# A second, transposed copy of the memory in a one-core encoder layer: its row factors spread by two matmuls with ones instead of sixteen transposes of its rows

## Chip, cores and metric

The kernel runs on one core of one Trainium2 chip. The metric is device time in microseconds (us) of one launch; less is better. Before the change three runs gave 854.33 to 855.25 us, median 854.94 us.

## What is computed

One layer of a bidirectional encoder trunk on 512 tokens of width 1024: token mixing (an attention group beside an HGRN2 group with gated scans), cross-attention into 256 memory tokens, a gated MLP with a convolution. Every sub-layer has an RMSNorm ahead and behind. Cut to the part that the change touches:

```
def rmsnorm(x, g):
    y = x * rsqrt(mean(x * x, axis=-1) + EPS)
    return y * g
...
m = rmsnorm(mem, mem_norm_g[l])                    # mem: 256 x 1024
x = x + rmsnorm(memory_cross_attention(h, m, w_xq[l], w_xkv[l], w_xo[l]), post_x_g[l])
...
kv = (m @ wkv)                                     # keys and values of the cross-attention
```

The whole program is one `layer` function in float32; products are kept at nearly float32 accuracy by splitting each operand into a rounded high part and a low part.

## The kernel before

**Products.** A projection multiplies activations by weight units of 128x1024. Every operand is held as a pair of fp32r tiles, high and low, made by `split` (lines 102 to 104): a copy on ACT (line 103) and a subtraction on DVE or POOL (line 104). `mm3` (lines 145 to 148) issues the three products high-high, high-low and low-high, so the lines 146, 147 and 148 of PE are the projections of the whole kernel. `issue` (line 115) loads a weight unit over SP and splits it, three units ahead of its use.

**Order.** The kernel is recorded in program order and a scheduler places the instructions on each engine by priorities and by its own idea of durations; every engine then runs its list strictly in order. `weave` (line 57) decides the recording order by shares: in the mixing stage (line 630) it interleaves `mix_projections` (line 607) with `cores` (line 618), the HGRN2 cores of heads 0 to 2. PE has the projections to do while a core's chain on DVE goes on.

**A core** (`hgrn_core`, line 439) begins with a sum of two key tiles on DVE (line 449) and four float32 matmuls on it (line 452). Then come levels m = 1, 2, 4, ... 64: ACT copies the keys (line 459), PE makes four float32 matmuls (line 462), DVE scales keys and queries in place (line 488, twice), multiplies decay factors (line 493) and merges the result under a mask (line 494). A level's matmuls need the DVE scalings of the level before and the ACT copy behind them. Its products go to the two PSUM banks of tag "c"; its copies use a ring of four tiles of tag "th" (`TMP_BUFS`, line 40).

**The memory.** `mem_norm` (line 592), called first in `mix_projections`, loads the gain row, spread over 128 partitions, and the two 128x1024 blocks of rows. `row_rstd` (line 197) squares and sums a block on ACT (line 199), POOL makes the reciprocal root (lines 164, 165), and `scale_rows` (line 180) multiplies rows by factor and gain on DVE in two halves (line 181, four instructions in all). `mem_turn` (line 602), called after the projections of head 2, transposes the 16 blocks of 128x128 on PE (`turn_in`, line 184; matmuls against the identity, line 190) in four groups of four, each into a PSUM bank of tag "b", and splits each bank into the pair `kv["m"]`, which the key and value projections of the cross-attention read much later. Right after it `mix_projections` goes on with the attention's keys and values (`put_kv`, line 555: rotary tables at lines 529 and 531, `vv` splits, `norm_rope`).

Of the kernel before, what the change touches and what calls it, by code (L numbers as in the profile page):

```python
# [9 lines left out]
F32 = mybir.dt.float32  # L10
F32R = mybir.dt.float32r
BF16 = mybir.dt.bfloat16
U8 = mybir.dt.uint8
ACT = mybir.ActivationFunctionType
ALU = mybir.AluOpType
# [3 lines left out]
P = 128  # L19
D = 1024  # L20
T = 512
NB = T // P
KC = D // P
M = 256
MB = M // P
# [48 lines left out]
def layer(tc, io, out):  # L74
    nc = tc.nc
    ctx = ExitStack()
    pool = lambda name, **k: ctx.enter_context(tc.tile_pool(name=name, **k))
    const = pool("const", bufs=1)
# [8 lines left out]
    def small():  # L87
        return sm.tile([P, 16], F32, name="small", tag="small")

    def bank(tag):  # L90
        return ps.tile([P, 512], F32, name="ps_" + tag, tag=tag)

    def big(shape, dt=F32):
        return b8.tile(shape, dt, name="big", tag="big")

    def tmp2(shape=(P, 512), dt=F32, tag="ta"):
        return t2.tile(list(shape), dt, name="tmp2", tag=tag, bufs=TMP_BUFS[tag])

    def tmp4(shape, dt=F32):
        return t4.tile(shape, dt, name="tmp4", tag="tmp4")  # L100

    def split(hi, lo, src, eng=None):
        nc.scalar.copy(hi, src)  # L103
        (eng or nc.vector).tensor_sub(lo, src, hi.bitcast(F32))  # L104
# [45 lines left out]
    def blk(b):  # L150
        return slice(b * P, (b + 1) * P)

    def rows_bc(src, n):
        return src[None, :].to_broadcast([P, n])

    def gains(*names, eng=None):
        g = big([P, 2, D])
        for i, name in enumerate(names):
            (eng or nc.gpsimd).dma_start(g[:, i, :], rows_bc(io[name], D))
        return [g[:, i, :] for i in range(len(names))]  # L160

    def rstd_of(ss, n, width):
        r = small()
        nc.gpsimd.tensor_scalar(r[:, :n], ss, 1.0 / width, EPS, op0=ALU.mult, op1=ALU.add)
        last_pow[0] = nc.gpsimd.tensor_tensor(out=r[:, :n], in0=r[:, :n], in1=nhalf[:, :n], op=ALU.pow).ins
        return r

    def half(c):
        return slice(c * 512, c * 512 + 512)
# [10 lines left out]
    def scale_rows(xb, r, g, h, c):  # L180
        nc.vector.scalar_tensor_tensor(out=h[:, half(c)], in0=xb[:, half(c)], scalar=r, in1=g[:, half(c)],
                                       op0=ALU.mult, op1=ALU.mult)

    def turn_in(h, act, b, tags, before=None):
        for c in range(2):
            if before:
                before(c)
            o = bank(tags[c]).rearrange("p (k n) -> p k n", k=4)
            for k in range(4):
                nc.tensor.transpose(o[:, k, :], h[:, blk(c * 4 + k)], ident)  # L190
            hi, lo = act.hi, act.lo
            if len(hi) == 2:
                split(hi[c][:, :, blk(b)], lo[c][:, :, blk(b)], o)
            else:
                split(hi[0][:, c * 4:c * 4 + 4, blk(b)], lo[0][:, c * 4:c * 4 + 4, blk(b)], o)

    def row_rstd(xb, h):
        ss = small()
        nc.scalar.activation(h, xb, ACT.Square, accum_out=ss[:, 0:1])
        return rstd_of(ss[:, 0:1], 1, D)[:, 0:1]  # L200
# [111 lines left out]
    ident = const.tile([P, P], F32, name="ident")  # L312
    g_row = tmp4([P, D])
    ones = const.tile([P, P], F32, name="ones")
# [28 lines left out]
    for b in range(NB):  # L343
        h = tmp4([P, D])
        if b == 0:
            ss = small()
# [3 lines left out]
            r = ss[:, R:R + 1]  # L350
        else:
            with tc.issue_after(last_pow[0]):
                r = row_rstd(x[b], h)
        for c in range(2):
            nc.vector.scalar_tensor_tensor(out=h[:, half(c)], in0=x[b][:, half(c)], scalar=r, in1=g_pre[c],
                                           op0=ALU.mult, op1=ALU.mult)
# [233 lines left out]
    kv = {}  # L590

    def mem_norm():
        g_mem, = gains("mem_norm_g")
        kv["rows"] = big([P, MB, D])
        for b in range(MB):
            m = kv["rows"][:, b, :]
            nc.gpsimd.dma_start(m, io["mem"][blk(b), :])
            r = row_rstd(m, tmp4([P, D]))
            for c in range(2):
                scale_rows(m, r, g_mem, m, c)  # L600

    def mem_turn():
        kv["m"] = Act([big([P, 8, M], F32R)], [big([P, 8, M], F32R)])
        for b in range(MB):
            turn_in(kv["rows"][:, b, :], kv["m"], b, "bb")

    def mix_projections():
        mem_norm()
        yield from proj_tm(hT, tm_tags, put_sg)
        yield from hgrn_in(1)  # L610
        yield from hgrn_in(2)
        mem_turn()
        yield from proj_tm(hT, tm_tags, put_kv, 256)
        late = []
        yield from proj_tm(hT, tm_tags, lambda b, z: late.append(lambda: put_qn(b, z)))
        yield from hgrn_in(3, late)
# [252 lines left out]
    for b in range(NB):  # L869
        ss, done = small(), []  # L870
# [99 lines left out]
```

## Time and profile before

| what | value |
|---|---|
| three runs, median (lowest to highest) | 854.94 us (854.33 to 855.25) |
| span of the profiled execution, first to last instruction | 852.5 us |
| median of the runs less that span | 2.4 us |
| PE busy | 832.2 us, 98% of the span |
| DVE busy | 516.3 us, 61% |
| ACT busy | 395.4 us, 46% |
| POOL busy | 104.8 us, 12% |
| DMA moved | 81.43 MB, mean 96 GB/s |

The page gives the profiled execution's span; of what lies around it the page has no figure of that execution alone, so sums are made against the span of 852.5 us, and the 2.4 us by which the median of the runs stands above it are added at the end. Times in rows count from the start of the span. In a row of a timeline the first number is the start, the second the time covered, then engine, line, operation, output<-input, shapes and count; brackets give the idle time ahead of it and what ended it. Matmuls are pipelined, so the distance of two starts, and not the printed duration, is what one of them costs PE.

### The profile page before, as it was taken

What the parts mean: (1) busy time and instruction counts of PE and PEld (TensorE: products, weight loads), DVE (VectorE), ACT (ScalarE), POOL (GpSimd) and SP (SyncE); (2) the same over time, 40 slices, a digit from 0 to 9 for tenths busy, and PEclk for the clock granted to TensorE, in tenths of its full rate; (3) what the DMA queues carried; (4) which work ended last, traced back from release to release, by engine and by line L of the source; (5) the groups of instructions that cost most, each with busy time, mean ns of one, the idle gap of its engine ahead of it and who ended that gap; (6) DMA issues with size and microseconds to landing.
All of it is one profiled execution on the core that took longest, in us unless ns stands there. A gap on an engine that the chain in (4) does not pass through costs nothing.

```text
span 852.5 us, 11064 instructions
## 1 busy us (share of the span) xinstructions
PE 832.2 (98%) x4324; PEld 703.2 (82%) x4324; DVE 516.3 (61%) x780; ACT 395.4 (46%) x701; POOL 104.8 (12%) x138
## 2 busy tenths in 40 slices
PE   6999999999999999999999999999999999999996
PEld 4878889887898888888888898888888888888885
DVE  4449487969997784864453765555555556822224
ACT  6353444444888874645543643333333335511121
POOL 5210300113334401300000400000000000000001
PEclk9999999999999999999999999999999999999999
DMA  6621212122222225152212142332322222322312
GB/s 210 220 100 50 75 49 88 50 75 75 67 82 75 75 73 200 58 190 75 83 47 93 54 145 100 99 99 99 100 99 99 99 93 81 101 97 99 99 49 100
DMA packets 23894, 81.43 MB, mean 96 GB/s; under 512 B 3041, under 2 KB 3681, under 8 KB 23842
## 3 DMA queue, kind: packets, MB, share of 16 engines
q1 hardware_dynamic: 22034, 75.35, 26.0%
q0 software_dynamic: 1232, 4.46, 1.6%
q10 hardware_dynamic: 576, 0.92, 0.3%
q8 instruction: 34, 0.56, 0.3%
q14 instruction: 18, 0.15, 0.1%
HBM read 78.61 MB, written 2.10 MB: 95 GB/s over the span
## 4 chain that ended last, share of the span: by engine, by line
PE 90%; DVE 6%; ACT 2%; issue 1%; POOL 1%; DMA 0%; POOLq 0%; DVEq 0%; SPq 0%; ACTq 0%
PE ps_b L146 9%; PE ps_b L147 9%; PE ps_b L148 9%; PE ps_s L148 6%; PE ps_s L146 6%; PE ps_s L147 6%; PE ps_o L146 6%; PE ps_o L148 6%; PE ps_o L147 6%; PE ps_c L146 4%; PE ps_c L148 4%; PE ps_c L147 4%; PE ps_c L462 3%; PE ps_o L683 2%; DVE big L488 1%; PE ps_o L671 1%
## 5 line engine op out<-in xcount | busy, mean ns | idle before, releaser
L104 DVE TENSOR_TENSOR wl<-raw,wh 128x1024 fp32r<-128x1024 f32 x114 | 139.5, 1223 | 230.7 <-ACT wh L103 230.5
L103 ACT CAST wh<-raw 128x1024 fp32r<-128x1024 f32 x130 | 136.8, 1052 | 252.5 <-PE ps_o L148 85.4
L146 PE MATMUL ps_b<-big,wh 128*128 128x512 f32 (+1 forms) x320 | 117.9, 368 | 0.0
L147 PE MATMUL ps_b<-big,wh 128*128 128x512 f32 (+1 forms) x320 | 116.6, 364 | 0.0
L148 PE MATMUL ps_b<-big,wl 128*128 128x512 f32 (+1 forms) x320 | 116.5, 364 | 0.0
L174 POOL TENSOR_SCALAR small<-small 128x1 f32<-128x1 f32 x42 | 14.4, 343 | 444.9 <-ACT tmp L205 421.7
L148 PEld LDWEIGHTS ps_b<-big,wl 128*128 128x128 f32 x320 | 60.3, 189 | 9.3
L147 PEld LDWEIGHTS ps_b<-big,wh 128*128 128x128 f32 x320 | 60.4, 189 | 9.0
L146 PEld LDWEIGHTS ps_b<-big,wh 128*128 128x128 f32 x320 | 60.3, 189 | 9.0
L146 PE MATMUL ps_s<-wh,big 128*128 128x512 f32 (+1 forms) x156 | 60.8, 390 | 1.7 <-ACT big L103 1.7
L148 PE MATMUL ps_s<-wh,big 128*128 128x512 f32 (+1 forms) x156 | 60.2, 386 | 0.0
L147 PE MATMUL ps_s<-wl,big 128*128 128x512 f32 (+1 forms) x156 | 60.0, 384 | 0.0
L146 PE MATMUL ps_o<-wh,big 128*128 128x512 f32 (+1 forms) x140 | 53.9, 385 | 0.0
L148 PE MATMUL ps_o<-wh,big 128*128 128x512 f32 (+1 forms) x140 | 53.4, 382 | 0.0
L147 PE MATMUL ps_o<-wl,big 128*128 128x512 f32 (+1 forms) x140 | 53.2, 380 | 0.0
L488 DVE TENSOR_TENSOR big<-big 128x512 f32<-128x512 f32 x64 | 49.8, 786 | 3.1 <-PE ps_c L462 1.2
L104 POOL TENSOR_TENSOR wl<-raw,wh 128x1024 fp32r<-128x1024 f32 x16 | 38.7, 2423 | 58.0 <-ACT wh L103 52.7
L104 DVE TENSOR_TENSOR big<-ps_o,big 128x512 fp32r<-128x512 f32 x52 | 35.7, 688 | 15.9 <-ACT big L103 15.6
L103 ACT CAST big<-ps_o 128x512 fp32r<-128x512 f32 x52 | 30.4, 585 | 19.8 <-PE ps_o L780 7.5
L146 PE MATMUL ps_b<-wh,big 128*128 128x512 f32 x92 | 36.7, 399 | 0.0
L147 PE MATMUL ps_b<-wl,big 128*128 128x512 f32 x92 | 36.1, 393 | 0.0
L148 PE MATMUL ps_b<-wh,big 128*128 128x512 f32 x92 | 35.9, 390 | 0.0
(227 smaller groups left out, 1840.6 us busy)
## 6 DMA issues: line engine op xcount, KB each, us to landing
raw<-in_w_dram SPq DMA_DIRECT2D x132, 512.0 KB, 3.2
big<-in_x_dram SPq DMA_DIRECT2D x7, 512.0 KB, 8.8
big<-in_mem_dram POOLq DMA_DIRECT2D x2, 512.0 KB, 7.0
out_dram<-big SPq DMA_DIRECT2D x4, 256.0 KB, 2.0
out_dram<-big ACTq DMA_DIRECT2D x3, 256.0 KB, 2.0
big<-in_x_dram SPq DMA_DIRECT2D x2, 256.0 KB, 2.9
big<-in_mem_norm_g_dram POOLq DMA_DIRECT2D x1, 512.0 KB, 6.2
big<-in_post_mix_g_dram POOLq DMA_DIRECT2D x1, 512.0 KB, 6.0
```

The lines of the kernel that those rows point to most:

```text
L103: nc.scalar.copy(hi, src)
L104: (eng or nc.vector).tensor_sub(lo, src, hi.bitcast(F32))
L146: nc.tensor.matmul(o, a[0], b[0], start=start, stop=False)
L147: nc.tensor.matmul(o, a[0], b[1], start=False, stop=False)
L148: nc.tensor.matmul(o, a[1], b[0], start=False, stop=stop)
L174: nc.gpsimd.tensor_scalar(ss[:, i + 4:i + 5], ss[:, i:i + 1], 1.0 / D, ss[:, i + 3:i + 4] if i else EPS, op0=ALU.mult, op1=ALU.add)
L462: nc.tensor.matmul(o[:, b, :], kc[:, blk(b)], pat(qk, b * P, [[2 * m, P // (2 * m)], [T + m, 2], [1, m]]), start=True, stop=True)
L488: nc.vector.tensor_tensor(out=c, in0=c, in1=pat(tt, toff + off, [[2, npair], [gap, 2], [0, m]]), op=ALU.mult)
L671: nc.tensor.transpose(o[:, c, :], e[:, 0, blk(c)], ident)
L683: nc.tensor.matmul(o, vv[:, c, h // 4].rearrange("p a d -> p (a d)"), pt[:, j, c, :], start=c + j == 0, stop=c == 3 and j == 1)
```

## The change

`mem_norm` now loads the memory twice, as rows and in transposed layout (`mt`, prepared on the host as 128 x 8 x 256), and the gain as a 128x8 column tile `gm` in place of the spread row. The sums of squares of both blocks go into one small tile and one pair of POOL instructions makes both factors. No row is scaled. `mem_turn` lets POOL write two diagonal matrices of the factors (`diag`, from the "th" ring), PE multiplies ones with them (two float32 matmuls, which leave the 256 factors on every partition), ACT copies the result to `wide` (also "th"), DVE multiplies each of the eight 128x256 pieces of `mt` by its gain column and `wide` in place, and two splits of 128x1024 make the pair.

```
     def mem_norm():
-        g_mem, = gains("mem_norm_g")
-        kv["rows"] = big([P, MB, D])
+        gm = const.tile([P, KC], F32, name="gm")
+        mt, rows = big([P, KC, M]), big([P, MB, D])
+        nc.gpsimd.dma_start(gm, io["gm"])
+        nc.gpsimd.dma_start(rows, io["mem"].rearrange("(b p) d -> p b d", p=P))
+        nc.gpsimd.dma_start(mt, io["mt"])
+        ss = small()
         for b in range(MB):
-            m = kv["rows"][:, b, :]
-            nc.gpsimd.dma_start(m, io["mem"][blk(b), :])
-            r = row_rstd(m, tmp4([P, D]))
-            for c in range(2):
-                scale_rows(m, r, g_mem, m, c)
+            nc.scalar.activation(tmp4([P, D]), rows[:, b, :], ACT.Square, accum_out=ss[:, b:b + 1])
+        r = rstd_of(ss[:, :MB], MB, D)
+        kv["rows"] = mt, gm, r
 
     def mem_turn():
-        kv["m"] = Act([big([P, 8, M], F32R)], [big([P, 8, M], F32R)])
+        mt, gm, r = kv["rows"]
+        m = big([P, 8, M], F32R), big([P, 8, M], F32R)
+        kv["m"] = Act([m[0]], [m[1]])
+        diag = tmp2((P, MB, P), tag="th")
         for b in range(MB):
-            turn_in(kv["rows"][:, b, :], kv["m"], b, "bb")
+            nc.gpsimd.tensor_scalar(diag[:, b, :], ident, r[:, b:b + 1], None, op0=ALU.mult)
+        o = bank("b")[:, :M]
+        for b in range(MB):
+            nc.tensor.matmul(o[:, blk(b)], ones, diag[:, b, :], start=True, stop=True)
+        wide = tmp2((P, M), tag="th")
+        nc.scalar.copy(wide, o)
+        for kc in range(KC):
+            nc.vector.scalar_tensor_tensor(out=mt[:, kc, :], in0=mt[:, kc, :], scalar=gm[:, kc:kc + 1], in1=wide,
+                                           op0=ALU.mult, op1=ALU.mult)
+        for c in range(2):
+            k = slice(4 * c, 4 * c + 4)
+            split(m[0][:, k, :], m[1][:, k, :], mt[:, k, :])
```

On the host `arrays["mt"]` and `arrays["gm"]` are added and `mem_norm_g` is dropped. In the changed file the lines behind the edit stand 16 lower.

The scheduler places other instructions differently too. Three places follow.

**DVE where the core of head 0 begins** (line 449 is its first step, line 181 scales the memory's rows), as a piece of the difference:

```order
-L181 SCALAR_TENSOR_TENSOR big<-big,small 128x512 x4
-L449 TENSOR_TENSOR tmp_515<-big 128x512
+L449 TENSOR_TENSOR tmp_508<-big 128x512
 L493 TENSOR_TENSOR big<-big 128x512
 L488 TENSOR_TENSOR big<-big 128x256x2
 L493 TENSOR_TENSOR big<-big 128x256
-L104 TENSOR_TENSOR wl<-raw,wh 128x1024
+L493 TENSOR_TENSOR big<-big 128x128
+L493 TENSOR_TENSOR big<-big 128x64
 L488 TENSOR_TENSOR big<-big 128x256x2
```

The four row scalings ahead of the core are gone, and a weight split (line 104) that stood inside its first level now stands two levels later. On PE the core's first matmuls (line 452) have moved up accordingly: they stood behind the 7th product of `put_sg`'s second weight unit, and now stand behind the 19th of the 24 products of its first.

**DVE where the core of head 2 begins**, `mem_turn`'s work just ahead of it. Before:

```order
L429 TENSOR_TENSOR big<-tmp_889,big 128x512
L104 TENSOR_TENSOR big<-ps_b,big 128x4x128 x2
L104 TENSOR_TENSOR big<-ps_c,big 128x512
L104 TENSOR_TENSOR big<-ps_b,big 128x4x128
L449 TENSOR_TENSOR tmp_1187<-big 128x512
L104 TENSOR_TENSOR big<-ps_b,big 128x4x128
L488 TENSOR_TENSOR big<-big 128x256x2
L493 TENSOR_TENSOR big<-big 128x512
L493 TENSOR_TENSOR big<-big 128x256
L488 TENSOR_TENSOR big<-big 128x256x2
```

And now (line 617 scales `mt`, the line 104 on 128x1024 with output `big` splits it, the line 104 on `ps_c` is an output of head 1's core):

```order
L429 TENSOR_TENSOR big<-tmp_882,big 128x512
L617 SCALAR_TENSOR_TENSOR big<-big,gm,tmp_1124 128x256 x8
L104 TENSOR_TENSOR big<-big 128x1024
L104 TENSOR_TENSOR big<-ps_c,big 128x512
L104 TENSOR_TENSOR big<-big 128x1024
L449 TENSOR_TENSOR tmp_1172<-big 128x512
L493 TENSOR_TENSOR big<-big 128x512
L488 TENSOR_TENSOR big<-big 128x256x2
L493 TENSOR_TENSOR big<-big 128x256
L104 TENSOR_TENSOR wl<-raw,wh 128x1024
L488 TENSOR_TENSOR big<-big 128x256x2
```

Ten instructions on the memory now stand ahead of the core's first step where three stood (a fourth stood behind it), and a weight split has come into its first level.

**PE in the core of head 2** (line 462 are the four matmuls of a level; the lines 146 to 148 on 128x256 are the products of `put_kv`'s projection). Before, the fourth level's neighbourhood:

```order
L146 MATMUL ps_o<-wh,big 128x256
L147 MATMUL ps_o<-wl,big 128x256
L462 MATMUL ps_c<-big,tmp_1386 128x128 x4
L148 MATMUL ps_o<-wh,big 128x256
L146 MATMUL ps_s<-wh,big 128x512
```

And now:

```order
L146 MATMUL ps_o<-wh,big 128x256
L147 MATMUL ps_o<-wl,big 128x256
L148 MATMUL ps_o<-wh,big 128x256
L462 MATMUL ps_c<-big,tmp_1227 128x128 x4
L462 MATMUL ps_c<-big,tmp_1325 128x128 x4
L462 MATMUL ps_c<-big,tmp_1371 128x128 x4
L146 MATMUL ps_s<-wh,big 128x512
```

Before, the 52 products of 128x256 that follow the core's line 452 were spread between its levels: 9 ahead of the second level, 19 ahead of the third, 23 ahead of the fourth, one behind. Now 40 of them stand ahead of line 452, 12 between the first and the second level, and none between the second, the third and the fourth.

## Rows read from the trace of the kernel before

**Rows 1.** The page, part 1: busy time of PE and DVE, share, count.
```profile
PE 832.2 (98%) x4324; PEld 703.2 (82%) x4324; DVE 516.3 (61%) x780; ACT 395.4 (46%) x701; POOL 104.8 (12%) x138
```
**Rows 2.** What PE waited for: us in total, times, longest.
```profile
PE ps_c L452 <- DVE tmp L449: 2.4, 2, 1.3
```
**Rows 3.** Windows: length, then busy (count) of PE, PEld, DVE, ACT, POOL, PEclk, DMA, GB/s.
```profile
60.00:80.00 20.00, 18.50 (x105) 15.24 (x105) 19.00 (x32) 7.06 (x10) 1.86 (x3) 1.00 0.15 50
...
140.00:160.00 20.00, 19.66 (x155) 18.67 (x154) 18.39 (x37) 9.92 (x18) 2.89 (x5) 1.00 0.20 67
```
**Rows 4.** Timeline of DVE where head 0's core begins.
```profile
58.80 0.69 DVE L429 TENSOR_TENSOR big<-tmp,big 128x512 f32<-128x512 f32 x1
60.21 1.41 DVE L181 SCALAR_TENSOR_TENSOR big<-big,small 128x512 f32<-128x512 f32 x2 [0.73 <-POOL small L165]
...
63.39 0.69 DVE L449 TENSOR_TENSOR tmp<-big 128x512 f32<-128x512 f32 x1
```
**Rows 5.** Timeline of PE in the same stretch.
```profile
59.82 0.39 PE L146 MATMUL ps_o<-wh,big 128*128 128x512 f32 x1
...
64.23 1.13 PE L452 MATMUL ps_c<-tmp,tmp 128*128 128x128 f32 x8 [1.30 <-DVE tmp L449]
...
66.38 0.53 PE L147 MATMUL ps_s<-wl,big 128*128 128x512 f32 x1
...
68.28 1.20 PE L462 MATMUL ps_c<-big,tmp 128*128 128x128 f32 x8 [0.21 <-DVE big L488]
```
**Rows 6.** Timeline of PE from the first memory transposes to the fourth level of head 2.
```profile
140.87 0.60 PE L190 MATMUL ps_b<-ident,big 128*128 128x128 f32 x4
...
148.19 1.16 PE L452 MATMUL ps_c<-tmp,tmp 128*128 128x128 f32 x8
149.19 1.49 PE L462 MATMUL ps_c<-big,tmp 128*128 128x128 f32 x8
150.38 0.42 PE L148 MATMUL ps_o<-wh,big 128*128 128x256 f32 x1
...
152.03 1.20 PE L462 MATMUL ps_c<-big,tmp 128*128 128x128 f32 x8 [0.28 <-DVE big L488]
...
156.15 0.36 PE L146 MATMUL ps_o<-wh,big 128*128 128x256 f32 x1
...
158.99 1.13 PE L462 MATMUL ps_c<-big,tmp 128*128 128x128 f32 x8
...
160.08 0.40 PE L146 MATMUL ps_s<-wh,big 128*128 128x512 f32 x1
```
**Rows 7.** Timeline of DVE from the first memory split to the rotary tables.
```profile
144.79 1.28 DVE L104 TENSOR_TENSOR big<-ps_b,big 128x512 fp32r<-128x512 f32 x2
...
147.46 0.68 DVE L449 TENSOR_TENSOR tmp<-big 128x512 f32<-128x512 f32 x1
...
153.27 0.69 DVE L488 TENSOR_TENSOR big<-big 128x512 f32<-128x512 f32 x1 [0.24 <-PE ps_c L462]
153.88 0.73 DVE L494 COPY_PREDICATED big<-masks,ps_c 128x512 f32<-128x512 uint8 x1
154.50 1.21 DVE L104 TENSOR_TENSOR wl<-raw,wh 128x1024 fp32r<-128x1024 f32 x1
155.63 0.42 DVE L529 TENSOR_TENSOR big<-big,qkg 128x256 f32<-128x256 f32 x1
```
**Rows 8.** Timeline of PE soon after the start.
```profile
13.39 1.12 PE L190 MATMUL ps_c<-ident,tmp 128*128 128x128 f32 x4 [0.77 <-DVE big L104]
...
15.59 0.63 PE L148 MATMUL ps_s<-wh,big 128*128 128x512 f32 x1
...
16.02 0.46 PE L146 MATMUL ps_s<-wh,big 128*128 128x512 f32 x1
```
**Rows 9.** The page, part 3: a queue of small transfers, packets, MB, share of 16 engines.
```profile
q10 hardware_dynamic: 576, 0.92, 0.3%
```
**Rows 10.** Timeline of POOL: its idle time after the start.
```profile
4.17 0.19 POOL L174 TENSOR_SCALAR small<-small 128x1 f32<-128x1 f32 x1 [2.73 <-ACT tmp L348]
```

More of the change, by code (lines that the diff above doesn't have):

```diff
@@ L952 @@
         arrays[name] = a[name][0]
+    arrays["mt"] = a["mem"][0].reshape(M, KC, P).transpose(2, 1, 0)
+    arrays["gm"] = a["mem_norm_g"][0].reshape(KC, P).T
+    del arrays["mem_norm_g"]
     arrays["hg_lb"] = a["hg_lb"].reshape(2, 2, 4, P).transpose(3, 0, 1, 2)
```

## The prediction

> **What bounds the kernel.** I read the page's busy times first: PE is busy for 832.2 of 852.5 us [rows 1], so time comes from two sources only, work that PE no longer does and the 20 us in which it waits. The list of what PE waited for comes next. Apart from the start, its longest entry is the first step of an HGRN2 core, where line 452 waits for DVE's line 449: 2.4 us in two waits [rows 2]. The windows say where DVE is the tight engine: from 60 to 80 us it is busy for 19.0 of 20 us and PE for 18.5, from 140 to 160 us DVE for 18.4 and PE for 19.7 [rows 3]. The first window holds the old row scalings, the second the old transposes; both are also where a core starts. So the change must be priced in two queues, PE's own and DVE's, and in the order in which the scheduler has put them together. The timelines of both places give the durations [rows 4 to 7]. All times below are on the clock of the profiled execution.
>
> **Term 1, PE's own work.** From the first group of transposes at 140.87 to line 452 at 148.19 PE spends 7.32 us [rows 6] on 38 products of 128x256, four groups of memory transposes and one like group of head 1 (the counts are from the order). A product costs 0.12 us: 23 of them lie between 156.15 and 158.99 [rows 6]. So 38 take 4.56, and the five groups 2.76, or 0.55 each with their gaps and changes of mode: the four that go save 2.2 us. The two new float32 matmuls of 128 columns have the price of line 452's four, 148.19 to 149.19 [rows 6]: 0.25 each, 0.6 with the change of mode. Net 1.6 us less. Their input `diag` is no wait: POOL writes it between the factors of head 0's core and those of head 1's, in an idle stretch of tens of us, and the ACT copy to `wide` stands ahead of anything DVE can reach.
>
> **Term 2, the start of head 0's core.** Before, DVE finished line 429 at 59.4, waited 0.73 us for POOL's factors, scaled rows, waited again and began line 449 only at 63.39 [rows 4]. PE stood 1.30 us at line 452 and 0.21 at the second level's line 462 [rows 5], 1.5 us in all. Now the scalings are gone, line 449 starts behind line 429 at 59.4 and ends at 60.1. The scheduler has moved line 452 forward to just behind the product that starts at 59.82, [rows 5], or 60.05 at twice 0.12 us for twice the columns: a wait of 0.1. Then the second level: from line 449 to it DVE took 63.39 to 68.28 [rows 4, 5], 4.9 us, with a weight split of 1.13 in it (154.50 to 155.63 is one [rows 7]); that split is now behind it, two short multiplications are in its place, so some 4.1 us and line 462 can start at 63.6. PE arrives at 60.1 + 2.15 (64.23 to 66.38 [rows 5]) + 4 products of 0.23 + 0.1 = 63.3: a wait of 0.3 to 0.5. Of 1.5 us of waits 0.6 or less are left: 0.9 us less, at least 0.4 (if the chain is as long as before) and at most 1.5 (if both waits go).
>
> **Term 3, the start of head 2's core.** Here the change adds DVE work. The old four splits took 0.60 each (two in 1.28, with 0.08 of overlap [rows 7]), three of them ahead of line 449. The new chain begins in the same place, 144.79: eight scalings of 128x256, two splits of 1.13 [rows 7] and the split of head 1 of 0.60. The scaling on 256 columns isn't in the trace. Above, it costs what 512 columns cost, 0.67 (1.41 for two [rows 4]), below 0.28; I take 0.34, which is half of the 512-column one and also the 0.42 less 0.08 of line 529 on 256 columns [rows 7]. So 144.79 + 2.7 + 1.1 + 0.6 + 1.1 = 150.4, 0.1 more for the ACT copy ahead of the second split, and line 449 ends near 151.2, where it ended at 148.1.
>
> PE gets to line 452 at 148.19 − 1.6 + 40 products of 0.12 = 151.4: no wait there. Line 452 and the first level take 2.19 (148.19 to 150.38 [rows 6]), the 12 products left 1.5: 155.1. The second level needs DVE: from line 449 at 147.46 to it at 152.03 took 4.57 [rows 6, 7]; a memory split of 0.60 leaves that stretch and a weight split of 1.13 enters, less up to 0.4 us in which DVE idled: 4.9 after 150.5 gives 155.3 to 155.4. From here on PE has nothing between the levels. From second level to third: line 462 at 152.03 released line 488 at 153.27, whose result came at 153.96 [rows 6, 7]; with 0.1 for the signal that is 2.05, so the third starts at 157.4, a wait of about 1.1 behind a level's 0.97 (158.99 to 160.08, less one product [rows 6]). From third to fourth: DVE does line 488 (0.61), line 494 (0.62), and then the same piece of queue as before, rotary tables, `vv` splits and both line 488, from 155.63 to at most 158.99 [rows 6, 7], 3.36. Line 488 starts 0.83 before the third level can. So the fourth starts 0.61 + 0.62 + 3.36 − 0.83 = 3.8 behind the third, at 161.2: a wait of 2.8. PE is through at 162.1, where it was at 160.08 [rows 6] with the same work done. Terms 1 and 3 together: 2.0 us more. Bounds: with scalings of 0.67 it is 4.6. Downward the scalings count little, since PE itself is at the second level only at 155.1 and the two waits behind it run from PE's own products through DVE and back; with that 0.3 and half a microsecond off the 3.36, which is an upper limit, 1.2 are left.
>
> What is late afterwards is everything, by the same amount: but for a few neighbours that change places until the end of that core, the order behind it is the old one on every engine, and DVE there runs behind PE's products.
>
> **Terms that I put at nothing.** The rows come in one transfer and the second copy adds 0.5 MB net, 5 us at the run's mean 96 GB/s. Its cover: both loads stand on POOL ahead of the factors that DVE awaited at 60 us [rows 4], but behind nothing that waits, and the copy is first read at 145. If the weight units beside it were late by all of that, and not one was ahead, it would cost those 5 us; three units are kept ahead, each worth 24 products of 0.23, so nothing is left of it. The gain tile `gm` is scheduled as POOL's first transfer, at about 1.4 us, ahead of the factors that start the kernel. POOL idles 2.73 us there [rows 10], so its issue is covered; its 128 short pieces share the DMA engines with the first rows of x. 576 packets of a small queue took 0.3% of 16 engines' span [rows 9], 41 us or 0.07 each; eight per engine would delay x by 0.6 us at most. I take 0.
>
> **Sum.** −0.9 + 2.0 = 1.1 us more than the span of 852.5, thus 853.6 and, with the 2.4 us around it, 856.0 against a median of 854.94: 0.13% slower. This kernel's measurement can tell 0.2%, 1.7 us, from no change, so this is the case "same". Its own range is 854.6 (1.2 and the whole 1.5) to 857.0.
>
> **Rivals.** *The clock falls* (slower). In the forecast PE waits 1.1 us, works 1 us, waits 2.8 us. The longest wait at a core's start was 1.3 us [rows 2], and the granted clock read 1.00 there, the 2.4 GHz level [rows 3]. Soon after the start products of 512 columns came 0.43 apart [rows 8], not 0.23: the 1.2 GHz level, whatever the clock row says of that stretch. If the waits near 158 and 161 us send PE there, a dense stretch like the one from 13.39 to 16.02 [rows 8], 2.6 us, loses half, 1.3, and the level in between up to 0.9: 857.3 to 858.2. It decides if the second wait is as long as worked out. The Trainium skill, "TensorE: Matmul & The Clock Gate", section "Why this matters for your kernels", says the same as a rule: products are to be issued back to back, and an idle gap of some length sends TensorE back to half rate. By that rule the change pays twice for its gap; no row of the old trace shows a gap that long behind a warm start.
>
> *The levels are covered after all* (faster). If PE found each level ready, terms 1 and 2 alone would be left: 854.94 − 1.6 − 0.9 = 852.4. Against it: DVE is busy for 18.4 of 20 us in that window [rows 3] and gets 2.6 us more, and from the second level on the waits don't depend on when DVE began. It decides only if DVE's pieces between two levels take less than a level of PE, 0.97.
>
> *The gain's pieces delay x*: 0.6 more, 856.6, still "same" unless term 3 is at its upper end. *It doesn't do what it says*: the order shows four groups of transposes less and two matmuls more, so only the gain can be missing, which is the forecast.
>
> **How the numbers follow.** Forecast 0.60, delayed x 0.08 (of the two together 0.05 passes the 0.2% bound), clock 0.17, a term 3 nearer to its upper end 0.09, levels covered 0.06. So faster 0.06, same 0.63, slower 0.31. The range reaches from the forecast's lower end, 854.6, to the clock's upper one, 858.2, and leaves out the covered levels and the far end of term 3.
>
> **What would show it.** Right: line 452's first wait of 1.30 us gone and the window of 60 to 80 us with PE near 19.4; the new matmuls at about 140; line 449 of head 2 three us later against the first split's place; two waits of PE for line 488, near 1 and 3 us, between the second and fourth level of head 2, near 157 and 161 us. Wrong: no wait above 1 us there, products more than 0.3 apart behind it, or a first product that starts later than before.

## The result and the profile after

The changed kernel takes 857.11 us (median of 8, 856.20 to 858.19), the kernel before beside it 854.55 (854.15 to 855.25): a ratio of 1.003, 95% interval 1.002 to 1.004. That is 2.6 us or 0.3% slower, more than the 0.2% that the prediction counted as no change, which is where the interval begins, and inside the range of 854.6 to 858.2. The likeliest case had said 856.0. What came is the rival "the clock falls", to which the prediction had given 0.17.

The profiled execution took 856.93 us with a span of 855.2. What lies around a span is 1.7 us here, and 1.8 in an execution of the kernel before for which both numbers are known (854.33 and 852.5). The 2.4 us that the prediction added came from a span and a median of different executions.

The page's first part after. PE's busy time is that of [rows 1], the span is 2.7 us longer:
```profile
span 855.2 us, 11037 instructions
PE 832.3 (97%) x4312; PEld 703.5 (82%) x4312; DVE 517.5 (61%) x782; ACT 395.3 (46%) x700; POOL 106.8 (12%) x138
```
What PE waited for, after (us in total, times, longest). Line 452 lost the wait of 1.3 [rows 2], line 462 has one of 2.6:
```profile
PE ps_c L462 <- DVE big L488: 4.5, 5, 2.6
...
PE ps_c L452 <- DVE tmp L449: 1.4, 2, 1.1
```
The windows after (columns as in [rows 3]): from 60 to 80 us PE gained 1.1 us, from 140 to 160 it lost 3.4, and from 160 to 180 the granted clock reads 0.91:
```profile
60.00:80.00 20.00, 19.58 (x115) 16.79 (x114) 17.23 (x30) 6.80 (x10) 2.15 (x2) 1.00 0.21 70
...
140.00:160.00 20.00, 16.27 (x128) 15.44 (x126) 19.77 (x38) 10.69 (x19) 0.85 (x2) 1.00 0.21 67
160.00:180.00 20.00, 19.74 (x109) 16.78 (x110) 17.92 (x48) 7.78 (x17) 4.68 (x8) 0.91 0.10 29
```
PE's timeline after, at head 0's and head 2's core. It answers to [rows 5, 6]:
```profile
60.27 1.13 PE L452 MATMUL ps_c<-tmp,tmp 128*128 128x128 f32 x8
...
64.05 1.20 PE L462 MATMUL ps_c<-big,tmp 128*128 128x128 f32 x8 [0.40 <-DVE big L488]
...
139.58 0.60 PE L613 MATMUL ps_b<-tmp,ones 128*128 128x128 f32 x4
139.94 0.36 PE L146 MATMUL ps_s<-wh,big 128*128 128x256 f32 x1
...
150.31 1.16 PE L452 MATMUL ps_c<-tmp,tmp 128*128 128x128 f32 x8 [0.27 <-DVE tmp L449]
...
154.45 1.20 PE L462 MATMUL ps_c<-big,tmp 128*128 128x128 f32 x8 [0.24 <-DVE big L488]
156.53 1.13 PE L462 MATMUL ps_c<-big,tmp 128*128 128x128 f32 x8 [0.88 <-DVE big L488]
160.26 1.55 PE L462 MATMUL ps_c<-big,tmp 128*128 128x128 f32 x8 [2.61 <-DVE big L488]
161.46 0.77 PE L146 MATMUL ps_s<-wh,big 128*128 128x512 f32 x1
162.03 0.63 PE L147 MATMUL ps_s<-wl,big 128*128 128x512 f32 x1
162.46 0.63 PE L148 MATMUL ps_s<-wh,big 128*128 128x512 f32 x1
```
Three waits of 0.24, 0.88 and 2.61 us ahead of the second, third and fourth level, near the forecast (0.2 to 0.3, 1.1, 2.8), and behind them products of 512 columns 0.43 us apart. Windows of 1 us after show why: the clock goes to its 1.2 GHz level some half a microsecond after the last wait ends, with the fourth level under way, and is back at 2.4 GHz near 164:
```profile
160.00:161.00 1.00, 0.74 (x6) 0.77 (x7) 1.00 (x6) 0.00 (x0) 0.88 (x2) 0.90 0.00 0
161.00:162.00 1.00, 1.00 (x5) 0.94 (x5) 1.00 (x4) 0.24 (x1) 0.00 (x0) 0.50 0.00 0
...
164.00:165.00 1.00, 1.00 (x5) 0.66 (x4) 1.00 (x5) 0.00 (x0) 0.48 (x1) 0.89 0.00 0
```
DVE's timeline after, from the scalings to line 449 of head 2 (it answers to [rows 7]) and at the fourth level:
```profile
143.53 3.25 DVE L617 SCALAR_TENSOR_TENSOR big<-big,gm,tmp 128x256 f32<-128x256 f32 x8
146.70 1.22 DVE L104 TENSOR_TENSOR big<-big 128x1024 fp32r<-128x1024 f32 x1
147.84 0.68 DVE L104 TENSOR_TENSOR big<-ps_c,big 128x512 fp32r<-128x512 f32 x1
148.44 1.22 DVE L104 TENSOR_TENSOR big<-big 128x1024 fp32r<-128x1024 f32 x1
149.57 0.68 DVE L449 TENSOR_TENSOR tmp<-big 128x512 f32<-128x512 f32 x1
...
158.64 0.68 DVE L488 TENSOR_TENSOR big<-big 128x512 f32<-128x512 f32 x1
...
159.44 0.68 DVE L488 TENSOR_TENSOR big<-big 128x512 f32<-128x512 f32 x1
```

Where the time went is read best from one instruction of PE in both traces:

| PE instruction | before | after | difference |
|---|---|---|---|
| line 190 in the first 25 us | 22.80 | 22.85 | +0.05 |
| first product of head 1's projection (line 146) | 92.59 | 91.35 | -1.24 |
| first product of 256 columns behind the new matmuls | 141.22 | 139.94 | -1.28 |
| first product of 512 columns behind the fourth level of head 2 | 160.08 | 161.46 | +1.38 |
| the seventh of these products | 161.46 | 164.26 | +2.80 |
| span | 852.5 | 855.2 | +2.7 |

1.3 us are won at head 0's core, 2.7 lost at head 2's, and 1.4 more over the next six products, at half the clock (0.1 of the 1.4 is a matmul of line 571 that stood later before). From there to the end the offset stays between 2.2 and 2.9 but for a few products that change places.

### The profile page after: what moved, and what is told of

It is laid out like the page before. It is cut to its first block, busy times and chain, and to the rows that moved or that the text cites. A ratio compares the mean times of both kernels' runs of the same rounds, so it can differ in the third digit from the quotient of the medians.

```text
span 855.2 us, 11037 instructions
## 1 busy us (share of the span) xinstructions
PE 832.3 (97%) x4312; PEld 703.5 (82%) x4312; DVE 517.5 (61%) x782; ACT 395.3 (46%) x700; POOL 106.8 (12%) x138
## 4 chain that ended last, share of the span: by engine, by line
PE 90%; DVE 7%; ACT 1%; issue 1%; POOL 0%; DMA 0%; POOLq 0%; DVEq 0%; SPq 0%; ACTq 0%
PE ps_b L146 9%; PE ps_b L147 9%; PE ps_b L148 9%; PE ps_s L148 7%; PE ps_s L146 7%; PE ps_s L147 7%; PE ps_o L146 6%; PE ps_o L148 6%; PE ps_o L147 6%; PE ps_c L146 4%; PE ps_c L148 4%; PE ps_c L147 4%; PE ps_c L462 3%; PE ps_o L699 2%; DVE big L488 2%; PE ps_o L687 1%
## 5 line engine op out<-in xcount | busy, mean ns | idle before, releaser
L462 PE MATMUL ps_c<-big,tmp 128*128 128x128 f32 x224 | 32.7, 290 | 4.5 <-DVE big L488 4.5
L146 PE MATMUL ps_b<-wh,big 128*128 128x512 f32 x92 | 36.6, 398 | 0.0
L462 PEld LDWEIGHTS ps_c<-big,tmp 128*128 128x128 f32 x224 | 29.6, 193 | 8.2 <-ACT tmp L459 5.1
```

Of the source, the lines that this page charges most:

```text
L146: nc.tensor.matmul(o, a[0], b[0], start=start, stop=False)
L462: nc.tensor.matmul(o[:, b, :], kc[:, blk(b)], pat(qk, b * P, [[2 * m, P // (2 * m)], [T + m, 2], [1, m]]), start=True, stop=True)
```

## The experiments

All times are medians; each series of kernels ran beside the kernel before on one chip.

| kernel | us | lowest to highest | ratio to before, 95% interval |
|---|---|---|---|
| after_again | 857.35 | 856.36 to 857.50 | 1.0031, 1.0020 to 1.0043 |
| fill8 | 856.22 | 855.52 to 857.02 | 1.0021, 1.0012 to 1.0029 |
| rope_early | 854.69 | 854.06 to 855.36 | 1.0003, 0.9994 to 1.0012 |
| turn_early | 854.60 | 853.49 to 854.98 | 0.9998, 0.9989 to 1.0007 |
| no_row_scale | 853.55 | 852.65 to 854.23 | 0.9986, 0.9977 to 0.9995 |
| gain_late | 857.53 | 856.96 to 858.52 | 1.0035, 1.0022 to 1.0047 |
| turn_early_diag | 853.70 | 852.97 to 854.29 | 0.9990, 0.9981 to 0.9999 |
| turn_early_diag_rope | 853.36 | 852.95 to 854.31 | 0.9986, 0.9977 to 0.9995 |
| half_scale | 854.55 | 853.94 to 855.65 | 1.0001, 0.9992 to 1.0010 |
| split_turn | 851.47 | 851.34 to 852.03 | 0.9966, 0.9954 to 0.9979 |

The kernel before stood at 854.36, 854.71 and 854.61 in the three series (first four, next four, last two rows).

**The two rivals on the clock.** The changed kernel again, and with the long wait filled:

> The changed kernel once more, for a second look at its clock and for a comparison beside the next three. Theory W (waits and clock): PE waits 0.2 to 0.3, 0.9 and 2.6 us for line 488 ahead of the second, third and fourth level of head 2, and the granted clock reads 0.50 for some us from the end of the longest wait on, near 161 us, as in the first profile (160.81 to 164.22). The offset of PE against the kernel before is +1.4 us at the first product behind the fourth level and +2.6 to +2.8 us from 165 us on. Time 857.1, 856.4 to 857.8. Rival S (the clock is chance): the waits are there, but no stretch of 0.50 at 161 us; the time is then 855.7 or, if it is still 857.1, the last 1.3 us come from somewhere else.

The waits are the same (4.5 us at line 462, longest 2.6), and the clock reads 0.91 again from 160 to 180. It did so in the profile of gain_late too: three profiled executions of three.

```
                 o = bank("c").rearrange("p (b n) -> p b n", b=NB)
+                if h == 2 and i == 3:
+                    for _ in range(8):
+                        nc.tensor.matmul(o.rearrange("p b n -> p (b n)"), hT.get(0, blk(0))[0], hT.get(0, slice(0, T))[0], start=True, stop=True)
                 for b in range(NB):
```


> The changed kernel with eight products of 512 columns put in front of the fourth level of head 2, into the bank that this level then overwrites; nothing else is moved. They take 8 x 0.23 = 1.8 us of the wait of 2.6. Theory W: DVE and the fourth level are as late as before, the wait that is left is 0.8, the granted clock reads 1.00 from 150 to 180 us, the products behind the level come 0.23 apart and not 0.43, and 1.4 us come back: 855.7, 855.2 to 856.2. Rival S (the clock does not hang on this wait, or costs nothing): 857.1, as the changed kernel. Rival D (the eight products delay what follows): 857.1 plus up to 1.8.

PE's timeline of fill8 (the fill is line 463, the levels are line 465):
```profile
157.79 1.13 PE L465 MATMUL ps_c<-big,tmp 128*128 128x128 f32 x8 [0.88 <-DVE big L491]
158.67 2.09 PE L463 MATMUL ps_c<-big 128*128 128x512 f32 x8
161.53 1.13 PE L465 MATMUL ps_c<-big,tmp 128*128 128x128 f32 x8 [0.77 <-DVE big L491]
162.41 0.48 PE L146 MATMUL ps_s<-wh,big 128*128 128x512 f32 x1
162.73 0.39 PE L147 MATMUL ps_s<-wl,big 128*128 128x512 f32 x1
162.96 0.40 PE L148 MATMUL ps_s<-wh,big 128*128 128x512 f32 x1
```
The fourth level is as late as before, but the products behind it come 0.23 apart and the clock reads 1.00 in every microsecond from 160 to 165. Useless work, put into a wait, made the kernel faster: 1.1 us by the medians, 1.4 forecast; the two intervals against the kernel before overlap, from 1.0020 to 1.0029. In the trace the gain is clearer: this execution was 1.2 us behind that of the changed kernel from 23 us on, and 0.3 ahead of it at 164, so the fall cost 1.5 us here. Nothing else of PE's order differs.

**What PE waits for between the levels.** The edit takes four multiplications out of DVE's queue between the third and the fourth level:
```
+        qkv["rope"] = rope_tables()
         yield from hgrn_in(2)
```
(`put_kv` no longer calls it.)

> The changed kernel with the rotary tables (lines 529 and 531, four multiplications, 1.33 us of DVE between the third and the fourth level of head 2) computed ahead of head 2's projection. PE's order at this place stays. Theory W: line 488 of the fourth level comes 1.3 us earlier, the wait of 2.6 falls to 1.3. If the clock then stays at 1.00, 1.3 + 1.4 = 2.7 us come back: 854.4; if it still falls, 1.3: 855.8. Rival P (the queue between the third and fourth level is not what PE waits for; banks or ACT are late next): the wait stays above 2 us and the time at 856.5 to 857.1.

PE's timeline of rope_early, third and fourth level:
```profile
155.99 1.13 PE L462 MATMUL ps_c<-big,tmp 128*128 128x128 f32 x8 [0.88 <-DVE big L488]
158.39 1.13 PE L462 MATMUL ps_c<-big,tmp 128*128 128x128 f32 x8 [1.27 <-DVE big L488]
159.28 0.48 PE L146 MATMUL ps_s<-wh,big 128*128 128x512 f32 x1
159.59 0.40 PE L147 MATMUL ps_s<-wl,big 128*128 128x512 f32 x1
```
The wait of 2.61 is 1.27, the clock stays at 1.00 here, and 2.7 us come back, 854.69 against 854.4 forecast. PE's order is that of the changed kernel throughout. The queue on DVE is what PE waits for, and the two losses go together: half of the wait took the fall of the clock with it.

**How much of it is the load of the scalings.** Half of them left out (`for kc in range(4)` at line 616):

> The changed kernel with four of the eight scalings of line 617 left out (half of the memory is then not normalised): 1.6 us of DVE less ahead of line 449 of head 2, the rest of the code as in the changed kernel. The scheduler then puts nine products of 256 columns between the second and third level of head 2 and four between the third and fourth. Theory W: the load on DVE is what set the order, so half of it halves the loss there: line 449 at about 148, the second wait 0.5, the third gone, the fourth 1.9 in place of 2.6, and PE is through with the core 1.3 to 1.6 us earlier; if the clock still falls behind 1.9 us, 855.7, if not, 854.3. Rival Q (the loss hangs on the place of mem_turn, not on its length): 857.

PE's timeline of half_scale:
```profile
152.52 1.20 PE L462 MATMUL ps_c<-big,tmp 128*128 128x128 f32 x8 [0.24 <-DVE big L488]
154.72 1.16 PE L462 MATMUL ps_c<-big,tmp 128*128 128x128 f32 x8
158.33 1.23 PE L462 MATMUL ps_c<-big,tmp 128*128 128x128 f32 x8 [1.99 <-ACT tmp L459]
159.25 0.74 PE L146 MATMUL ps_s<-wh,big 128*128 128x512 f32 x1
159.79 0.63 PE L147 MATMUL ps_s<-wl,big 128*128 128x512 f32 x1
160.22 0.63 PE L148 MATMUL ps_s<-wh,big 128*128 128x512 f32 x1
```
The third level's wait is gone and the fourth's is 1.99, ended here by ACT's copy of line 459, which starts at 157.66 behind a weight cast and ends 0.3 us after DVE's second line 488; the clock falls behind that wait too (products 0.43 apart, 0.50 from 160 to 162 us). The load sets the order, and the order the waits. With the clock down I had expected 855.7; the median is 854.55, 2.6 to 2.8 us under the two series of the changed kernel, while the trace shows PE only 1.6 us earlier than there (from -0.4 at 23 us to -2.0 at 320). Whether the clock stayed up in other executions (two of the eleven stood near 855.6, the rest from 853.9 to 854.8) one profile doesn't tell: that part of the gain is not explained.

**The gain at head 0's core alone.** From the kernel before, the two lines `for c in range(2): scale_rows(...)` are taken out of `mem_norm`:

> The kernel before, its memory rows loaded and their factors computed as ever, but not multiplied by factor and gain (four scalings of line 181 less); the transposes of the rows and their splits stay as before. It leaves the memory's normalisation out. Theory W: this is the change's gain at head 0's core alone. PE's offset against the kernel before goes from 0 to -1.2 or -1.3 us between 60 and 80 us and stays there to the end; head 2's core looks as before (products between the levels, waits of 0.3); no stretch of 0.50 near 161 us. 854.4 - 1.25 = 853.1, 852.7 to 853.5. Rival G (the gain at head 0 is caught up by DVE later, as 1.1 us of an earlier delay were caught up at 221 us in another run): 854.4.

1.2 us faster by the median, and PE's offset is -1.07 at the product that stood at 77.34 before and -1.22 at 168.61. The gain is real and lasts.

**The start.** The gain's transfer behind the memory's:
```
-        nc.gpsimd.dma_start(gm, io["gm"])
         nc.gpsimd.dma_start(rows, io["mem"].rearrange("(b p) d -> p b d", p=P))
-        nc.gpsimd.dma_start(mt, io["mt"])
+        late_mt = nc.gpsimd.dma_start(mt, io["mt"])
+        with tc.issue_after(late_mt.ins):
+            nc.gpsimd.dma_start(gm, io["gm"])
```


> The changed kernel with the transfer of the gain tile put behind the two memory transfers in POOL's queue, in place of ahead of everything; PE's and DVE's orders stay. Theory X (the gain's 128 short pieces delay the first rows of x): PE's first 25 us come earlier by 0.3 to 0.8 us on the average and the time falls to 856.4 to 856.9, from 857.2. Theory W says nothing of the start: if the gain's transfer is hidden, 856.9 to 857.5, and the spread of the first 25 us from execution to execution stays near 1 us.

857.53: nothing came back, so the transfer at the start is not a visible part of the loss. The orders did not quite stay: one group of transposes near 20 us (line 190) moved by four products, and two pairs of DVE's instructions changed places. An effect of less than about half a microsecond could not be told in this series of five.

**The work where DVE is idle.** Four steps, each aimed at a wait that the one before had left:
```
+        mem_turn()
         yield from hgrn_in(1)
         yield from hgrn_in(2)
-        mem_turn()
```


> The changed kernel with mem_turn called ahead of hgrn_in(1) in place of behind hgrn_in(2): the eight scalings and both splits run where DVE has idle time (93 to 99 us), and none of them is left ahead of head 2's core. Theory W: line 449 of head 2 comes early again, the products of 256 columns lie between the levels as in the kernel before, no wait over 0.9 us is left there and no stretch of 0.50; the gains stay, 1.3 us at head 0's core and 1.6 us of PE's work; at the new place DVE holds line 512 of head 0 back, a wait of 0.4 to 1.0 of PE at line 516. 854.55 - 2.9 + 0.4 to 1.0 gives 852.4, 851.8 to 853.2. Rival O (the new load is paid for wherever it stands): the waits move to line 516 and to the next levels, 3 us or more, 855 to 857.

Right at head 2 (longest wait 0.52, clock 1.00) and wrong in the time: 854.60, where 852.4 was expected. PE's and POOL's timelines of turn_early:
```profile
92.35 0.49 PE L613 MATMUL ps_b<-tmp,ones 128*128 128x128 f32 x2
93.99 0.49 PE L613 MATMUL ps_b<-tmp,ones 128*128 128x128 f32 x2 [1.16 <-POOL tmp L610]
```
```profile
89.04 2.65 POOL L408 TENSOR_TENSOR tmp<-tmp,og 128x512 f32<-128x512 f32 x2 [1.39 <-ACT tmp L406]
91.68 2.25 POOL L610 TENSOR_SCALAR tmp<-ident,small 128x128 f32<-128x128 f32 x2
```
I had priced DVE's queue at the new place and not POOL's: the two diagonals, 1.1 us each, stand behind `put_sg`'s multiplications, and PE waits for the second one.

```
-        kv["rows"] = mt, gm, r
+        diag = kv["diag"] = rows[:, :, 0:P]
+        for b in range(MB):
+            nc.gpsimd.tensor_scalar(diag[:, b, :], ident, r[:, b:b + 1], None, op0=ALU.mult)
+        kv["rows"] = mt, gm, r
```


> mem_turn ahead of hgrn_in(1), as in turn_early, and the two diagonal tiles written by POOL right behind the factors of the memory rows (near 62 us, into the rows' own tile, which nobody reads any more) in place of at 91.7 us behind POOL's work for put_sg. Theory W: the wait of PE of 1.16 us at line 613 goes, the rest is as in turn_early: 854.6 - 1.2 = 853.4, 852.9 to 853.9. Rival N (a wait at the next place takes over: line 146 of head 1 or line 516, held back by DVE's scalings): 854.2 to 854.8.

> The same, and the rotary tables ahead of head 1's projection too, so that DVE's queue between the third and fourth level of head 2 is 1.3 us shorter. Theory W: these waits are already short once the products lie between the levels (0.5 us at most in turn_early), so the tables bring only 0.2 to 0.4: 853.1, 852.5 to 853.7. Rival T (the tables are worth their 1.3 us here as well): 852.1.

853.70 and 853.36; by the medians the tables bring 0.3 here, where the products lie between the levels (the two ranges overlap almost wholly), and 2.7 where they didn't. Both are faster than the kernel before, by 0.1%, but a wait has taken the place of the one removed. PE's and DVE's timelines of turn_early_diag:
```profile
99.05 0.33 PE L516 MATMUL ps_c<-ident,tmp 128*128 128x128 f32 x1 [1.18 <-DVE tmp L512]
```
```profile
94.08 0.35 DVE L512 SCALAR_TENSOR_TENSOR tmp<-ps_c,small,big 128x128 f32<-128x128 f32 x1 [1.53 <-POOL small L165]
94.35 3.25 DVE L618 SCALAR_TENSOR_TENSOR big<-big,gm,tmp 128x256 f32<-128x256 f32 x8
97.51 1.22 DVE L104 TENSOR_TENSOR big<-big 128x1024 fp32r<-128x1024 f32 x1
98.65 0.35 DVE L512 SCALAR_TENSOR_TENSOR tmp<-ps_c,small,big 128x128 f32<-128x128 f32 x1
```
The new work stands between the first and the second of four instructions that PE awaits. So it was cut up:
```
-        mem_turn()
-        yield from hgrn_in(1)
+        mem_spread()
+        yield from hgrn_in(1, [lambda: None, lambda: None, mem_turn(0), lambda: None, mem_turn(1)])
```
(`mem_spread` holds the two matmuls and the copy to `wide`, `mem_turn(c)` makes four scalings and a split. The rotary tables, ahead of `hgrn_in(1)` in turn_early_diag_rope, stand ahead of `mem_norm` here.)

> turn_early_diag_rope with mem_turn cut up: the two matmuls with ones and ACT's copy ahead of hgrn_in(1) (the copy goes into the rows' tile), the scalings and splits as two jobs between the parts of hgrn_in(1). On DVE all four of line 512 of head 0 now stand ahead of the first scaling, and the splits behind line 104 of that head. Theory W: the wait of 1.2 us of PE at line 516, which took the place of the one at line 613, goes, and nothing new comes: 853.4 - 1.2 = 852.2, 851.7 to 852.8, faster than the kernel before by 0.2 to 0.3%. Rival N (again a wait at the next place): 853.0 to 853.6.

DVE's timeline of split_turn:
```profile
94.14 1.13 DVE L512 SCALAR_TENSOR_TENSOR tmp<-ps_c,small,big 128x128 f32<-128x128 f32 x4 [1.52 <-POOL small L165]
95.19 3.25 DVE L619 SCALAR_TENSOR_TENSOR big<-big,gm 128x256 f32<-128x256 f32 x8
```
851.47 us, 0.34% faster than the kernel before (3.1 us) and by the medians 0.7% faster than the changed one: better than the forecast range, and the best kernel here. In the traces PE gains 1.5 us on turn_early_diag_rope between 92 and 103 us, where line 516 waited 1.2, and nothing more by 180 us, so the tables' other place is not what made it faster. Its span is 849.6, 2.9 us less than before: about what the two gains alone come to, 1.3 and 1.6, though the tables' place may have a share of 0.3 in it.

**The kernel before once more.**

> The kernel before once more, for one look. Theory W: no wait over 1.3 us of PE near 161 us and a granted clock of 1.00 there, as in the first profile. In three variants of the changed kernel the clock read 0.50 for 3.4 us near 211 to 217 us, at the waits of 1.4 and 1.6 us of PE there, which the kernel before has as well; if that comes and goes by chance, it may be seen here. Time 854.4, 853.8 to 855.4.

854.01 us; the clock reads 1.00 in the windows from 140 to 180 and from 200 to 220.

## Why the prediction was right in its range and wrong in its likeliest case

- **Term 1** (1.6 us of PE's work less) holds. After the change PE takes 10.73 us from the new matmuls to line 452 (139.58 to 150.31); without the wait of 0.27 and the 40 further products at 0.12 us that is 5.7, where it was 7.32 [rows 6]: 1.7 less. The two new matmuls cost 0.36 from start to start (139.58 to 139.94), or 0.45 with the change of mode behind them, not 0.6. Split_turn, which has the work without the long waits, is 2.9 us shorter in span, of which 1.3 are head 0's.
- **Term 2** (0.9 less, bounds 0.4 and 1.5) measured 1.2 to 1.3. The wait at the second level came as worked out (0.40, in the 0.3 to 0.5); line 452 found its input ready, where 0.1 of waiting was put down.
- **Term 3 with term 1** (2.0 more, bounds 1.2 and 4.6) measured 2.7, from -1.28 to +1.38. The mis-sized price is the scaling on 256 columns: 0.40 from start to start (143.53 to 146.70 for eight), against 0.34, half of the 512-column one. That is 0.5 us on eight and puts a wait of 0.27 at line 452, where none was expected. 0.2 of the rest is the fourth level itself, 1.20 to the next product instead of 0.97, already at the falling clock. Mechanism and places were right: order without products between the levels, three waits growing towards the fourth.
- **The clock** is where the likeliest case failed. The prediction worked out the 2.8 us, put the fall behind them as a rival and gave it 0.17; the row that spoke against it was a granted clock of 1.00 through waits of up to 1.3 us. The wait worked out was twice as long as any in that row, so it spoke for little. Rope_early bears the old evidence out (1.27 us, no fall), and half_scale and the changed kernel show the other side (1.99 and 2.61, a fall each). No run sets a threshold between them. The price of 1.3 to 2.2 us was right: 1.3 behind the level and 0.3 in it (1.20 to the next product, against 0.89 in rope_early), and 1.5 by the traces of fill8. The Trainium skill, "TensorE: Matmul & The Clock Gate", section "Why this matters for your kernels", has the rule that products are to be issued back to back because an idle gap of some length sends TensorE back to half rate. The gap that it names is longer than the 2.8 worked out and than the 1.99 and 2.61 behind which the clock fell here, so the rule as it stands did not foretell this fall; the measurement decides. Its direction fill8 bears out: the wait filled, no fall.
- **What lies around the span** was taken as 2.4 and is 1.8. It worked against the two misses: 852.5 + 2.7 + 1.8 would have been 857.0.
- **The gain's pieces** (0.6 us, 0.08) did not show in gain_late. **Levels covered** (852.4) was ruled out rightly for this order; split_turn reached it with another.
- The change does what it says, and what it saves is real: 2.9 us. Against split_turn it loses 5.6 us (857.1 and 851.5) by where its work on DVE, the diagonals and the rotary tables stand.

## What to carry to other kernels

When a change moves work from the engine that is full to one that is nearly so, read in the new order what stands behind the moved work, there and on every engine that feeds it; each of three places tried here turned one engine's queue into PE's wait, until the work was cut up. A wait of the matrix engine that is longer than any in the old trace is to be priced with the clock behind it as the likely case, not the rival. Taking half of such a wait away can return more than its length.

## What the runs showed that was not expected

- The first 25 us differ from execution to execution. The same instruction of PE (22.85 after) stood at 22.26 in rope_early, at 23.65 in turn_early and at 24.16 in fill8, though PE's order up to there is the same in all four, and the first waits vary with it. A single profile is not to be compared with another on its span without this offset.
- A second fall of the clock came in three of the thirteen profiles (fill8, rope_early, turn_early_diag), near 211 to 217 us, behind a wait of PE of 1.6 us at line 582 (581 or 585 in some variants) that all thirteen have: in the kernel before it is 1.54, and the clock stays at 1.00. So a wait of this length went either way, and it, not the 1.3 us at a core's start, is the longest that the old trace has after the start without a fall. The windows of rope_early:
```profile
210.00:212.00 2.00, 2.00 (x11) 1.66 (x10) 1.45 (x3) 1.11 (x2) 0.00 (x0) 0.69 0.02 4
212.00:214.00 2.00, 2.00 (x13) 1.90 (x13) 0.00 (x0) 1.97 (x3) 0.84 (x1) 0.50 0.04 8
```
 It cost 1.4 us on the spot and 0.3 to 0.5 in the end: at 218 us PE waits for DVE's line 449 in any case, 1.10 in the kernel before and 0.20 here.
```profile
218.08 1.16 PE L452 MATMUL ps_c<-tmp,tmp 128*128 128x128 f32 x8 [0.20 <-DVE tmp L449]
```
 So this fall cost what the next wait didn't swallow, 1.4 less 0.9. In the changed kernel the wait at this place was 1.12 us with all its delay: DVE was late there too. Why this second fall comes in some executions and not in others was not tried.
